# Three padding tiles move the weight buffers and the operands that meet them to other byte offsets

## The chip, the cores and the metric

One core of one Trainium2 chip runs the whole program in one launch. The metric is the device time of one execution in microseconds. Before the change it is 1166.29 us, the median of 3 runs (1164.71 to 1167.49). TensorE (PE in the profile) multiplies matrices, ScalarE (ACT) and VectorE (DVE) work element by element, GpSimd (POOL) does small things, and SyncE (SP) issues the weight loads.

## The reference

One layer on 256 tokens of width 2048. A combined projection of the normalised input feeds three branches, whose gated outputs are merged and projected:

```python
def hybrid_layer(x, mem, norm_g, w_in, ...):
    h = rms_norm(x, norm_g)
    proj = h @ w_in                                   # 2048 -> 16512 columns
    (aq, ak, av, az, br, bk, bv, bz, bwd, bad, cq, cz, ga, gb, gc) = jnp.split(proj, offsets, axis=-1)
    ya = chunked_band_attention(rms_norm(aq), rms_norm(ak), av, a_rel_bias) * jax.nn.silu(az)
    yb = rwkv7_time_mix(br, bk, bv, bwd, bad, ...) * jax.nn.silu(bz)
    mk, mv = jnp.split(rms_norm(mem, mem_norm_g) @ w_mem_kv, 2, axis=-1)
    yc = memory_cross_attention(rms_norm(cq), rms_norm(mk), mv) * jax.nn.silu(cz)
    merged = (jax.nn.sigmoid(ga) * (ya @ w_up_a) + jax.nn.sigmoid(gb) * (yb @ w_up_b)
              + jax.nn.sigmoid(gc) * (yc @ w_up_c))
    return x + merged @ w_o
```

All of it is float32. Nearly all of the arithmetic is in the products with weights: `w_in`, `w_mem_kv`, the three `w_up` and `w_o`.

## The kernel before

**The weight stream.** All weights are laid out in HBM as 185 chunks of 128 partitions by 2048 floats, in the order in which they are used. `wload` (L170) loads a chunk of 1 MB into `raw` (two buffers). `wchunk` (L183) turns each half of it into two tiles of the type float32r: ScalarE copies it to `whi` (L191), which rounds, and VectorE writes the rest, `raw - whi`, to `wlo` (L193). There are four buffers of each. Activations are split in the same way into a high and a low tile: `mh`, `ml` (the memory tokens), `xh`, `xl` (the input), `yth`, `ytl` (the outputs of branches A and C), `yh`, `yl` (of branch B) and `gh`, `gl` (the merged branches).

**The products.** Each product is three matmuls, high by high, low by high and high by low. A matmul has a stationary operand, which a weight load (LDWEIGHTS, PEld in the profile) puts into the array, and a moving operand, which streams through it. There are two forms.
- `proj` (L197; `proj_last`, L220, for the last output block) keeps the activations stationary, 128 columns at a time, and lets 512 columns of the weights stream: L210, L211 and L215, twelve matmuls to one half of a chunk.
- `proj_cm` (L251) is the other way round: 128 columns of the weights are stationary and 256 columns of the activations stream (L259, L260, L262).

Each matmul has a weight load of its own, as no two neighbours share the stationary operand. In a row of the profile such as `pp<-whi,xh` the names are the accumulator and the two operands.

**The order.** The order is that of the code. `spawn` and `tick` let the small work (attention, the RWKV recurrence, transposes) run as generators that take a step after every few matmuls. These small matmuls (L344, L493 and others) have ordinary float32 operands, not float32r.

**Where a tile lies.** A tile lies at the same byte offset in each of the 128 partitions. Pools hand out offsets one after another, in steps of 32 bytes, some from the left end of the partition and some (`side="right"`) from the right end. So an unused tile moves all that is handed out behind it. In the pools `const` (vectors and constants), `wts` (`raw`, `whi`, `wlo`) and `small` the order is const, wts, small, and behind them comes `xT` (`xh`, `xl`) and all else on the left. Buffers of one pool, and the columns that a matmul takes of a tile, are multiples of 512 bytes apart for all operands named above, so an operand's offset modulo 256 is the same in all its matmuls.

Of the kernel before, what the change touches and what calls it, by code (L numbers as in the profile page):

```python
# [18 lines left out]
P = 128  # L19
# [71 lines left out]
def build(nc, tc, A, out, dbg=None):  # L91
    dbg = dbg or {}
    ctx = ExitStack()
    with ctx:
        _build(ctx, nc, tc, A, out, dbg)


def _build(ctx, nc, tc, A, out, dbg):
    uid = [0]

    def nm(s):
        uid[0] += 1
        return f"{s}_{uid[0]}"

    def pool(st, name, bufs=1, side=None, space=None):
        kw = {}
        if side:
            kw["side"] = side
        if space is not None:
            kw["space"] = space  # L110
        return st.enter_context(tc.tile_pool(name=name, bufs=bufs, **kw))
# [3 lines left out]
    cp = pool(ctx, "const")  # L115
    wp = pool(ctx, "wts")
    sm = pool(ctx, "small")
# [4 lines left out]
    def t(pl, shape, tag, dtype=F32, bufs=1):  # L122
        return pl.tile(shape, dtype, name=nm(tag), tag=tag, bufs=bufs)
# [141 lines left out]
        return acc  # L265


    vec = t(cp, [P, NV], "vec")
    cst = t(cp, [P, NCST], "cst")
    ident = cst[:, C_ID:C_ID + P]  # L270
# [119 lines left out]
            yield 1  # L390


    xp = ExitStack()
    xpool = pool(xp, "xT")
    xh = t(xpool, [P, 16, S], "xh", F32R)
    xl = t(xpool, [P, 16, S], "xl", F32R)

    yc_st = ExitStack()
    ycp = pool(yc_st, "yc", side="right")
    ych = t(ycp, [P, 8, S], "yth", F32R)  # L400
# [722 lines left out]
```

## Time and profile before

| | |
|---|---|
| median of 3 runs | 1166.29 us |
| the profiled execution | 1162.67 us, of which the span from first to last instruction is 1160.9 |
| PE busy | 1141.2 us (98%), 6610 matmuls |
| PEld busy | 961.0 us (83%), beside PE |
| DVE, ACT, POOL busy | 804.7 (69%), 528.9 (46%), 167.5 (14%) |
| granted TensorE clock | 0.998 of 2.4 GHz on average |
| DMA | 212.75 MB, 183 GB/s on average |

PE's busy time is the union of matmuls that overlap, since a matmul is in flight longer (390 ns and more for 512 columns) than the distance at which the next one starts. So neither busy time nor the mean duration of a matmul says how fast TensorE gets on: that is read from the start times of neighbours in the timeline, and called spacing below.

### The profile page before, as it was taken

What the parts mean: (1) busy time and instruction counts of PE and PEld (TensorE: products, weight loads), DVE (VectorE), ACT (ScalarE), POOL (GpSimd) and SP (SyncE); (2) the same over time, 40 slices, a digit from 0 to 9 for tenths busy, and PEclk for the clock granted to TensorE, in tenths of its full rate; (3) what the DMA queues carried; (4) which work ended last, traced back from release to release, by engine and by line L of the source; (5) the groups of instructions that cost most, each with busy time, mean ns of one, the idle gap of its engine ahead of it and who ended that gap; (6) DMA issues with size and microseconds to landing.
All of it is one profiled execution on the core that took longest, in us unless ns stands there. A gap on an engine that the chain in (4) does not pass through costs nothing.

```text
span 1160.9 us, 16874 instructions
## 1 busy us (share of the span) xinstructions
PE 1141.2 (98%) x6610; PEld 961.0 (83%) x6610; DVE 804.7 (69%) x1378; ACT 528.9 (46%) x655; POOL 167.5 (14%) x232
## 2 busy tenths in 40 slices
PE   7999999999999999999999989899999999999998
PEld 6888989889889778988997779787788877888887
DVE  6874566556869667979786778956687956557443
ACT  6764545443643434444553634642553443444332
POOL 0100000034010204010214110213201203300000
PEclk9999999999999999999999999999999999999999
DMA  7765535466474654464644355554355574554663
GB/s 266 245 227 203 186 137 181 155 200 208 154 241 151 203 184 145 167 203 170 204 160 145 111 178 205 165 179 148 128 195 199 185 233 145 195 196 159 230 236 109
DMA packets 36905, 212.75 MB, mean 183 GB/s; under 512 B 5086, under 2 KB 7390, under 8 KB 13274
## 3 DMA queue, kind: packets, MB, share of 16 engines
q1 hardware_dynamic: 29664, 198.59, 49.9%
q0 software_dynamic: 3936, 9.44, 3.0%
q10 hardware_dynamic: 3226, 3.65, 1.0%
q8 instruction: 52, 0.85, 0.3%
q14 instruction: 27, 0.22, 0.1%
HBM read 206.95 MB, written 3.67 MB: 181 GB/s over the span
## 4 chain that ended last, share of the span: by engine, by line
PE 82%; DVE 9%; DMA 4%; issue 2%; ACT 1%; POOL 1%; SPq 0%; ACTq 0%; POOLq 0%; DVEq 0%
PE pp L210 21%; PE pp L211 20%; PE pp L215 20%; PE pp L259 4%; PE pp L260 4%; PE pp L262 4%; DVE wlo L193 3%; DMA raw<-in_wstream_dram 3%; DVE Xu L743 1%; DVE tmu L741 1%; DMA Tu<-scrt 1%; PE pp L232 1%; PE pp L234 1%; PE pp L231 1%; ACT whi L191 1%
## 5 line engine op out<-in xcount | busy, mean ns | idle before, releaser
L193 DVE TENSOR_TENSOR wlo<-raw,whi 128x1024 fp32r<-128x1024 f32 x368 | 455.8, 1250 | 255.4 <-ACT whi L191 254.3
L191 ACT CAST whi<-raw 128x1024 fp32r<-128x1024 f32 x368 | 380.2, 1051 | 533.4 <-PE pp L211 230.4
L210 PE MATMUL pp<-whi,xh 128*128 128x512 f32 x768 | 309.2, 403 | 1.5 <-ACT whi L191 1.5
L211 PE MATMUL pp<-whi,xl 128*128 128x512 f32 x768 | 300.8, 392 | 0.0
L215 PE MATMUL pp<-wlo,xh 128*128 128x512 f32 x768 | 206.6, 391 | 3.9 <-DVE wlo L193 3.9
L210 PEld LDWEIGHTS pp<-whi,xh 128*128 128x128 f32 x768 | 144.5, 188 | 35.8 <-ACT whi L191 3.0
L215 PEld LDWEIGHTS pp<-wlo,xh 128*128 128x128 f32 x768 | 144.2, 188 | 36.0 <-DVE wlo L193 5.9
L211 PEld LDWEIGHTS pp<-whi,xl 128*128 128x128 f32 x768 | 144.9, 189 | 28.6 <-issue 0.5
L259 PE MATMUL pp<-xh,whi 128*128 128x256 f32 x528 | 131.3, 287 | 0.0
L260 PE MATMUL pp<-xl,whi 128*128 128x256 f32 x528 | 129.6, 284 | 0.0
L259 PEld LDWEIGHTS pp<-xh,whi 128*128 128x128 f32 x528 | 101.2, 192 | 1.1 <-issue 0.6
L260 PEld LDWEIGHTS pp<-xl,whi 128*128 128x128 f32 x528 | 101.4, 192 | 0.6 <-issue 0.2
L262 PE MATMUL pp<-xh,wlo 128*128 128x256 f32 x528 | 74.1, 283 | 0.0
L262 PEld LDWEIGHTS pp<-xh,wlo 128*128 128x128 f32 x528 | 68.1, 192 | 0.0
L210 PE MATMUL pp<-whi,mh 128*128 128x512 f32 x128 | 50.9, 397 | 3.8 <-ACT whi L191 2.0
L210 PE MATMUL pp<-whi,yth 128*128 128x512 f32 x128 | 51.9, 405 | 0.0
L211 PE MATMUL pp<-whi,ytl 128*128 128x512 f32 x128 | 50.5, 395 | 0.0
L211 PE MATMUL pp<-whi,ml 128*128 128x512 f32 x128 | 50.1, 391 | 0.2 <-DVE ml L309 0.2
L741 DVE TENSOR_TENSOR tmu<-Tu,Xu 128x112 f32<-128x112 f32 (+29 forms) x124 | 32.6, 263 | 13.5 <-DMA Tu<-scrt 10.4
L210 PE MATMUL pp<-whi,gh 128*128 128x512 f32 x96 | 37.5, 390 | 0.0
L211 PE MATMUL pp<-whi,gl 128*128 128x512 f32 x96 | 37.4, 389 | 0.0
L215 PE MATMUL pp<-wlo,yth 128*128 128x512 f32 x128 | 35.0, 396 | 0.0
(258 smaller groups left out, 1346.3 us busy)
## 6 DMA issues: line engine op xcount, KB each, us to landing
raw<-in_wstream_dram SPq DMA_DIRECT2D x184, 1024.0 KB, 5.0
xraw<-in_xT_dram SPq DMA_DIRECT2D x8, 256.0 KB, 4.8
Tu<-scrt POOLq DMA_DIRECT2D x4, 512.0 KB, 4.6
xr<-in_x_dram POOLq DMA_DIRECT2D x8, 256.0 KB, 5.3
xraw<-in_memT_dram SPq DMA_DIRECT2D x7, 256.0 KB, 5.6
out_dram<-xr POOLq DMA_DIRECT2D x6, 256.0 KB, 3.4
bias<-in_rel_dram POOLq DMA_DIRECT2D x4, 256.0 KB, 3.7
tmpA<-in_bc_dram ACTq DMA_DIRECT2D x8, 128.0 KB, 4.3
```

The lines of the kernel that those rows point to most:

```text
L191: SC.copy(hi, sl)
L193: V.tensor_tensor(out=lo, in0=sl, in1=hi.bitcast(F32), op=ALU.subtract)
L210: T.matmul(acc[tt], xh[:, kt + k2, sl], hv[:, k2], start=(kt + k2 == 0), stop=False)
L211: T.matmul(acc[tt], xl[:, kt + k2, sl], hv[:, k2], start=False, stop=False)
L215: T.matmul(acc[tt], xh[:, kt + k2, sl], lv[:, k2], start=False, stop=(last and k2 == 1))
L231: T.matmul(acc, xh[:, kt + k2, sl], hv[:, k2, cs], start=(kt + k2 == 0), stop=False)
L232: T.matmul(acc, xl[:, kt + k2, sl], hv[:, k2, cs], start=False, stop=False)
L234: T.matmul(acc, xh[:, kt + k2, sl], lv[:, k2, cs], start=False, stop=(kt + k2 == nk - 1))
L259: T.matmul(acc, hv[:, k2], xh[:, kt + k2, :], start=(kt + k2 == 0), stop=False)
L260: T.matmul(acc, hv[:, k2], xl[:, kt + k2, :], start=False, stop=False)
L262: T.matmul(acc, lv[:, k2], xh[:, kt + k2, :], start=False, stop=(kt + k2 == 15))
L741: V.tensor_tensor(out=tv, in0=Tu[:, s, s + 1:32].unsqueeze(2).to_broadcast([P, n, m]), in1=X[:, s:s + 1, 0:m].to_broadcast([P, n, m]), op= ...
```

## The change

Three tiles that nothing reads or writes are added: 96 bytes at the head of `const`, 64 bytes at the end of `small`, and 32 bytes at the right end of the partition, ahead of the pool of `yth` and `ytl`.

```diff
+    t(cp, [P, 24], "padw")
     vec = t(cp, [P, NV], "vec")
     cst = t(cp, [P, NCST], "cst")
 ...
+    t(sm, [P, 16], "padx")
     xp = ExitStack()
     xpool = pool(xp, "xT")
     xh = t(xpool, [P, 16, S], "xh", F32R)
     xl = t(xpool, [P, 16, S], "xl", F32R)
 
+    padp = pool(ctx, "padr", side="right")
+    t(padp, [P, 8], "padr")
     yc_st = ExitStack()
     ycp = pool(yc_st, "yc", side="right")
     ych = t(ycp, [P, 8, S], "yth", F32R)
```

In the built programs the instructions of every engine are the same, in the same order, with the same shapes, waits and semaphore updates. What differs is the byte offsets. Modulo 256 they are:

| tiles | before | after |
|---|---|---|
| `raw`, `whi`, `wlo` | 160 | 0 |
| `xh`, `xl`, `mh`, `ml`, `gh`, `gl`, `yh`, `yl` | 160 | 64 |
| `xraw`, `merged`, `vL` and other tiles of the left side | 160 | 64 |
| `yth`, `ytl`, `mkT`, `mv`, `cqT` | 224 | 192 |
| the RWKV tiles `AX`, `BK`, `Tu`, `Xu` | 224 | 192 |
| `cst` (identity, masks), `eye8`, `warm` | 0 | 96 |
| the RWKV tiles `w2a2`, `rk0` | 0 | 224 |

So where a weight tile meets `xh`, `mh`, `gh` or `yh`, the two offsets are 160 and 160 before, and 0 and 64 after. Where it meets `yth` they are 160 and 224 before, and 0 and 192 after.

## Rows read from the trace of the kernel before

**Rows 1.** The profiled page: busy us (share of the span) xinstructions
```profile
PE 1141.2 (98%) x6610; PEld 961.0 (83%) x6610; DVE 804.7 (69%) x1378; ACT 528.9 (46%) x655; POOL 167.5 (14%) x232
```

**Rows 2.** The page's chain that ended last, by engine
```profile
PE 82%; DVE 9%; DMA 4%; issue 2%; ACT 1%; POOL 1%; SPq 0%; ACTq 0%; POOLq 0%; DVEq 0%
```

**Rows 3.** Waits of PE: engine line waited for: us in total, times, longest
```profile
PE pp L215 <- DVE wlo L193: 3.9, 3, 2.8
PE pp L210 <- ACT whi L191: 3.5, 2, 2.0
```

**Rows 4.** Waits of all engines, same columns
```profile
DVE wlo L193 <- ACT whi L191: 254.3, 174, 5.7
ACT whi L191 <- PE pp L211: 230.4, 138, 4.4
ACT whi L191 <- DMA raw<-in_wstream_dram: 213.9, 76, 8.7
```

**Rows 5.** Groups by shape: line engine op out<-in xcount | busy, mean ns | idle before
```profile
L210 PE MATMUL pp<-whi,xh 128*128 128x512 f32 x768 | 309.2, 403 | 1.5 <-ACT whi L191 1.5
L259 PE MATMUL pp<-xh,whi 128*128 128x256 f32 x528 | 131.3, 287 | 0.0
L210 PE MATMUL pp<-whi,yth 128*128 128x512 f32 x128 | 51.9, 405 | 0.0
L210 PE MATMUL pp<-whi,mh 128*128 128x512 f32 x128 | 50.9, 397 | 3.8 <-ACT whi L191 2.0 <-ACT mh L308 0.9 <-ACT whi L451 0.9
L210 PE MATMUL pp<-whi,gh 128*128 128x512 f32 x96 | 37.5, 390 | 0.0
L210 PE MATMUL pp<-whi,yh 128*128 128x512 f32 x64 | 25.2, 394 | 0.0
L231 PE MATMUL pp<-whi,gh 128*128 128x256 f32 x32 | 8.3, 282 | 0.0
L231 PE MATMUL pp<-whi,gh 128*128 128x512 f32 x16 | 6.3, 392 | 0.0
```

**Rows 6.** Timeline of PE, `proj` on `xh`: start us, us, engine line op xcount
```profile
880.11 0.39 PE L210 MATMUL pp<-whi,xh 128*128 128x512 f32 x1
880.34 0.39 PE L211 MATMUL pp<-whi,xl 128*128 128x512 f32 x1
...
881.47 1.07 PE L215 MATMUL pp<-wlo,xh 128*128 128x512 f32 x4
882.38 0.39 PE L210 MATMUL pp<-whi,xh 128*128 128x512 f32 x1
```

**Rows 7.** Timeline of PE, `proj` on `yth`
```profile
890.62 0.40 PE L210 MATMUL pp<-whi,yth 128*128 128x512 f32 x1
890.86 0.39 PE L211 MATMUL pp<-whi,ytl 128*128 128x512 f32 x1
891.09 0.40 PE L210 MATMUL pp<-whi,yth 128*128 128x512 f32 x1
...
893.42 0.40 PE L210 MATMUL pp<-whi,yth 128*128 128x512 f32 x1
```

**Rows 8.** Timeline of PE, from `proj` to `proj_cm`, and on in it
```profile
257.67 1.07 PE L215 MATMUL pp<-wlo,xh 128*128 128x512 f32 x4
258.58 0.28 PE L259 MATMUL pp<-xh,whi 128*128 128x256 f32 x1
258.69 0.28 PE L260 MATMUL pp<-xl,whi 128*128 128x256 f32 x1
...
259.77 0.28 PE L259 MATMUL pp<-xh,whi 128*128 128x256 f32 x1
...
260.49 0.88 PE L262 MATMUL pp<-xh,wlo 128*128 128x256 f32 x6
```

**Rows 9.** Timeline of PE, two runs of float32 matmuls
```profile
58.68 1.03 PE L344 MATMUL ps<-cst,qn 128*128 128x128 f32 x8
147.91 3.62 PE L493 MATMUL ps<-mkT,cqT 128*128 128x256 f32 x16
```

**Rows 10.** Groups: one of the float32 matmuls, and the two casts
```profile
L493 PE MATMUL ps<-mkT,cqT 128*128 128x256 f32 x32 | 7.2, 379 | 0.0
L344 PE MATMUL ps<-cst,qn 128*128 128x128 f32 x64 | 8.3, 273 | 0.0
L191 ACT CAST whi<-raw 128x1024 fp32r<-128x1024 f32 x368 | 380.2, 1051 | 533.4 <-PE pp L211 230.4 <-DMA raw<-in_wstream_dram 213.9 <-PE pp L260 39.2
L193 DVE TENSOR_TENSOR wlo<-raw,whi 128x1024 fp32r<-128x1024 f32 x368 | 455.8, 1250 | 255.4 <-ACT whi L191 254.3
```

**Rows 11.** The page's DMA issues: op xcount, KB each, us to landing
```profile
raw<-in_wstream_dram SPq DMA_DIRECT2D x184, 1024.0 KB, 5.0
```

## The prediction

> **What bounds the kernel now.** I read the page's busy shares first: TensorE is busy 98% of the span, the next engine 69% [rows 1]. Then what TensorE waits for: 3.9 us for `wlo` and 3.5 us for `whi` in 1160.9 [rows 3], while ScalarE waits 230.4 us for TensorE to free a `whi` buffer [rows 4]. So the weight feed is ahead, and the time is the sum of the distances at which matmuls start. The chain agrees with a reservation: 82% of it is PE, and 13% is DVE and DMA, places where the feed or the RWKV chain sets the pace [rows 2].
>
> Busy means of single matmuls (403 ns) overlap and say nothing of the spacing, so I read that from start times in the timeline.
> - `proj` on `xh`: ten matmuls from 880.11 to 882.38, 2.27/10 = 227 ns [rows 6].
> - `proj` on `yth`: twelve from 890.62 to 893.42, 2.80/12 = 233.3 ns, alternately about 240 and 230 as printed [rows 7].
> - `proj_cm`: six from 259.77 to 260.49, 120 ns [rows 8].
> - float32 matmuls of 256 columns: 16 in 3.62 us, (3.62 - 0.379)/15 = 216 ns; of 128 columns: (1.03 - 0.273)/7 = 108 ns [rows 9, 10].
>
> Two sizes give a slope and a fixed part. float32r: (227 - 120)/256 = 0.418 ns a column, so 107 ns for 256 columns and 214 for 512, and a fixed part of 13 ns for each matmul. float32: 108/128 = 0.84 ns a column, twice the slope, with a fixed part of 0 to 2 ns. All of them have a weight load each. And the `yth` matmuls, same shape and same moving tiles, have a fixed part of 19 ns. What differs there is the stationary offset, 224 where `xh` has 160. So the fixed part of a float32r matmul depends on where its operands lie; that is the one quantity which this change can move.
>
> **The change part by part.** No instruction, wait or order changes, so nothing is queued behind anything new. The three tiles cost no instruction. What is left is four kinds of access at new offsets.
>
> *float32r matmuls.* Each count is that of the high-by-high line times three lines. On `xh`, `mh`, `gh`, `yh`: (768 + 128 + 96 + 64 + 16) x 3 = 3216 with 512 columns. On `yth`: 128 x 3 = 384. With 256 columns: (528 + 32) x 3 = 1680 [rows 5]. In all 5280. The trace of before holds the offset pairs (160, 160) and (160, 224), and not (0, 64) or (0, 192), so the new fixed part is bounded from both sides. The low end is that of float32, 2 ns [rows 9]. The high end is that of `yth`, 19 ns [rows 7], for the new pairs too are 64 apart modulo 128. Within a stage the fixed part is not always 13: the first `proj_cm` matmul after a `proj` stage has a spacing of 0.11 us, a fixed part of 3 to 6, before 0.12 sets in [rows 8]. So 13 is not a floor of the float32r form; it comes from how the moving reads and the weight load fall on each other. Before, both offsets are odd multiples of 32 bytes; after, both are multiples of 64, a kind of pair that no row shows. I take 6 ns, the row nearest between the ends (107 + 6 = 113, which prints as 0.11). Gain: 7 ns x (3216 + 1680) = 34.3 us, and (19 - 6) x 384 = 5.0 us for `yth`, in all 39.3 us.
>
> Of this I let 85% reach the end, since 82% of the chain is PE [rows 2] and the stages in which something else sets the pace don't gain: 33.4 us. The feed covers the rest: a chunk is 24 matmuls, 24 x 0.220 = 5.28 us instead of 24 x 0.227 = 5.45, against 2 x 1.051 us on ScalarE, 2 x 1.250 us on VectorE [rows 10] and 5.0 us to land with two buffers in flight [rows 11]. What would be late next is the `raw` load, by way of VectorE, which has to free the buffer.
>
> *Casts and weight DMA.* ScalarE and VectorE read `raw` at 0 instead of 160, and DMA writes it there. No row shows what an offset does to them. Bound: TensorE waits 7.4 us for both casts [rows 3], so no more than that can be won; a loss would first use up ScalarE's 230.4 us of waiting [rows 4]. I take 0.
>
> *float32 matmuls.* There are 6610 - 5280 = 1330 records [rows 1]. Their fixed part is 0 to 2 ns at the pairs that `L344` (identity at 0, `qn` at 160) and `L493` (224 and 224) have [rows 9], so offsets have not mattered to them. I take 0; at the worst they would get the 13 ns of the others, 1330 x 11 = 15 us.
>
> *Element-wise work.* RWKV and attention tiles move by 32, 96 or 160 bytes; hidden as long as TensorE is 98% busy, 0.
>
> The sum against the profiled execution, 1162.67 us (span 1160.9): 1162.67 - 33.4 = 1129.3. The median of the runs shown lies 3.6 us above that execution, so the forecast is 1133 us on the median's scale.
>
> **What the skill says.** The rows have `yth` 6 ns slower than `xh` for nothing but its offset [rows 6, 7]. The Trainium skill, "TensorE: Matmul & The Clock Gate", "Step-by-step: what each phase is for", says that the moving operand and the weight load have two independent read ports, so that loading the next weights takes nothing from the running matmul; "SBUF — State Buffer", "SBUF: two separate sides", that PE never waits on another engine's port. By that an offset could not matter and the change would do nothing, a rival below; this trace does not agree, as 19 is not 13.
> The same TensorE page, "Wait — 56ns, not 53.3ns?", gives a spacing of N/2.4 + 2.5 ns at full clock, 215.8 for 512 columns. Only the float32 rows here are that close to their slope. An estimate by it: 11 ns off each of 4896 and 17 off each of 384, some 60 us, the floor among the rivals.
>
> **The rivals.**
> - *Floor.* The new offsets take away the whole collision, and float32r gets the fixed part of float32, 2 ns [rows 9]: 11 x 4896 + 17 x 384 = 60.4 us, of which 51 at 85%: 1115; all of it, 1106. For it: the float32 matmuls have weight loads too and no such cost. Against: they stream at half the pace, so they leave more room.
> - *Only the distance counts.* What matters is the difference of the two offsets, and 64 is the slow one. Then every matmul on `xh`, `mh`, `gh`, `yh` gets what `yth` has, 6.3 ns more: 3216 x 6.3 = 20.3 us, TensorE being the bound almost throughout: 1186; if the 256-column ones pay it too, another 10.6 us, 1197. For it: this is the only dependence that the trace shows directly. Against: it says nothing of why the pair (160, 160), with no distance at all, costs 13 ns. It decides as soon as the mean spacing on `xh` exceeds 227 ns.
> - *Nothing, or `yth` alone.* The 13 ns belong to the form, and only `yth`, whose tiles now have the offset distance of -64, changes: at most 384 x 6.3 = 2.4 us, so 1164 to 1166. For it: in all stages on `mh`, `xh`, `gh` the spacing is 227, however different the work beside them. Against: the 0.11 us at a stage's start [rows 8]. That the change doesn't do what it says is this case too: offsets move, and the array doesn't notice.
>
> **How the numbers follow.** Forecast 36%, floor 20%, distance 32%, nothing or `yth` alone 12%. Faster by over 0.2% (2.3 us, about what a measurement of this kernel can tell from none) are the forecast, the floor and a sixth of the last: 0.58. Slower is the distance: 0.32. The same: 0.10. The signs are mixed, so the range has to reach across: from 1104, the floor with all of it passed on, to 1190, the distance paid by the wide matmuls with 4 us for the unknown offsets of the casts. It leaves out the distance paid in full (about 8%) and a little below. The forecast's own range is 1120 to 1145, from a fixed part of 3 ns to one of 9.
>
> **What would show it.** In the profile after: the spacing of `L210` and `L211` on `xh` (220 ns if right, 216 by the floor, 233 by the distance, 227 by nothing), of `L259` (113, 109, up to 126, 120), and of `yth` equal to that of `xh`. The float32 rows stay at 216 and 108. TensorE's waits for `wlo` and `whi` grow from 7.4 us if the feed takes part of the gain. The prediction is wrong if the spacing rises, or if it falls and the span doesn't; a changed duration of the casts with unchanged spacing would mean that I looked at the wrong access.

## The result, and the profile after

The changed kernel takes 1173.44 us, the median of 4 runs (1171.67 to 1176.71), against 1165.5 us (1164.5 to 1167.49) for the kernel before, run beside it. The ratio is 1.0083, with a 95% interval of 1.0063 to 1.0104: it is slower by 0.8%, which is 9.7 us (7.3 to 12.1). The forecast, 1133 us, had the wrong sign.

The profiled execution took 1176.71 us, with a span of 1174.9 where before has 1160.9. Its page, first the busy shares (as [rows 1]), then the chain (as [rows 2]), the two casts (as [rows 10]) and the weight load (as [rows 11]):

```profile
PE 1156.2 (98%) x6610; PEld 959.5 (82%) x6610; DVE 805.1 (69%) x1378; ACT 529.3 (45%) x655; POOL 167.7 (14%) x232
...
PE 87%; DVE 6%; DMA 3%; ACT 1%; issue 1%; POOL 1%; SPq 0%; ACTq 0%; DVEq 0%; POOLq 0%
...
L193 DVE TENSOR_TENSOR wlo<-raw,whi 128x1024 fp32r<-128x1024 f32 x368 | 455.7, 1249 | 268.9 <-ACT whi L191 266.1
L191 ACT CAST whi<-raw 128x1024 fp32r<-128x1024 f32 x368 | 380.1, 1049 | 548.1 <-PE pp L211 262.5
...
raw<-in_wstream_dram SPq DMA_DIRECT2D x184, 1024.0 KB, 5.0
```

PE is busy 15.0 us longer with the same 6610 matmuls, the weight loads 1.5 us less, and every other engine as long as before, to 0.5 us. The casts and the weight load take what they took. TensorE's waits for the weights, as in [rows 3] (engine, line, what it waited for: us in total, times, longest):

```profile
PE pp L215 <- DVE wlo L193: 3.6, 3, 2.7
...
PE pp L210 <- ACT whi L191: 3.4, 2, 1.9
```

That is 7.0 us against 7.4. The casts, as in [rows 4], wait longer for TensorE and less for DMA:

```profile
DVE wlo L193 <- ACT whi L191: 266.1, 177, 5.6
ACT whi L191 <- PE pp L211: 262.5, 146, 4.6
ACT whi L191 <- DMA raw<-in_wstream_dram: 189.2, 72, 8.7
```

ScalarE's wait for a `whi` buffer grew from 230.4 to 262.5 us. So the feed is as far ahead as it was, and TensorE itself is slower. The timeline of PE in the changed kernel (start us, us, line, operands, count) shows at which matmuls: `proj_cm`, `proj` on `xh` and `proj` on `yth`, where [rows 8, 6, 7] show them before.

```profile
263.14 0.28 PE L259 MATMUL pp<-xh,whi 128*128 128x256 f32 x1
263.26 0.28 PE L260 MATMUL pp<-xl,whi 128*128 128x256 f32 x1
...
265.02 0.28 PE L262 MATMUL pp<-xh,wlo 128*128 128x256 f32 x1
...
888.86 0.39 PE L210 MATMUL pp<-whi,xh 128*128 128x512 f32 x1
889.09 0.40 PE L211 MATMUL pp<-whi,xl 128*128 128x512 f32 x1
...
890.73 0.86 PE L215 MATMUL pp<-wlo,xh 128*128 128x512 f32 x3
...
900.00 0.39 PE L210 MATMUL pp<-whi,yth 128*128 128x512 f32 x1
...
902.75 0.39 PE L210 MATMUL pp<-whi,yth 128*128 128x512 f32 x1
```

- `proj_cm`: 16 matmuls from 263.14 to 265.02, 117.5 ns each, where it was 120.
- `xh`: 8 from 888.86 to 890.73, 234 ns, where it was 227.
- `yth`: 12 from 900.00 to 902.75, 229 ns, where it was 233.3.

The means over all neighbours of a family, taken from the start times of the whole trace with pauses left out, give the account (a family has its high and its low tile):

| matmuls | count | before, ns | after, ns | change, us |
|---|---|---|---|---|
| on `xh`, `mh`, `gh`, `yh`, 512 columns | 3216 | 227.7 | 233.3 | +18.0 |
| on `yth`, 512 columns | 384 | 233.4 | 229.3 | -1.6 |
| `proj_cm`, 256 columns | 1584 | 119.9 | 117.8 | -3.3 |
| last block, 256 columns | 96 | 119.5 | 113.8 | -0.5 |
| sum | | | | +12.6 |

The spans differ by 14.0 us. The rest is about the clock: the mean granted clock of the execution is 0.996, and 0.998 before, which makes, as an estimate, 1174.9 x 0.004 - 1160.9 x 0.002 = 2.4 us. The windows show two places where the array now runs for a while at 1.2 of its 2.4 GHz and before did not. One lies between 700 and 800 us (mean clock 0.98, before 1.00), the other at the start (columns: stretch; its us, busy us and instructions of PE, PEld, VectorE, ScalarE and GpSimd, the granted clock, DMA share, GB/s). After:

```profile
14.00:16.00 2.00, 0.68 (x3) 0.20 (x2) 0.88 (x3) 1.43 (x2) 0.00 (x0) 1.00 0.99 244
16.00:18.00 2.00, 1.38 (x6) 1.16 (x7) 1.97 (x4) 2.00 (x4) 0.00 (x0) 1.00 0.89 319
18.00:20.00 2.00, 2.00 (x7) 1.52 (x6) 2.00 (x4) 1.12 (x3) 0.00 (x0) 0.51 0.79 280
20.00:22.00 2.00, 2.00 (x8) 1.58 (x7) 1.00 (x3) 0.55 (x1) 0.00 (x0) 0.63 0.84 269
```

Before, the same stretches:

```profile
14.00:16.00 2.00, 1.01 (x5) 0.51 (x3) 0.92 (x3) 1.05 (x2) 0.00 (x0) 1.00 0.83 267
16.00:18.00 2.00, 1.00 (x4) 0.86 (x5) 1.93 (x3) 2.00 (x4) 0.00 (x0) 1.00 0.92 317
18.00:20.00 2.00, 2.00 (x10) 1.65 (x9) 2.00 (x4) 1.51 (x4) 0.00 (x0) 1.00 0.66 243
```

In both, TensorE works 2.0 to 2.1 us of the 4 ahead of it (0.68 + 1.38, and 1.01 + 1.00); the clock falls to 0.51 in the one and stays at 1.00 in the other. This part does not belong to the offsets: in the last experiment below, whose matmuls on `mh` lie as before, the clock falls in the same stretch (0.57 from 18 to 20 us), and another execution of the changed kernel had a mean clock of 1.000 and a span of 1169.9, where 1160.9 - 2.3 + 12.6 = 1171.2 would be expected.

The float32 matmuls are where they were [rows 9]: eight in 1.03 us, though the distance of their operands (stationary less moving offset; here the identity moves) went from 160 to -32, and sixteen in 3.61, where both stay at one offset. In the fourteen traces of this document, which have distances of 0, 64, 160 and 224 modulo 256 there, the spacing of these transposes (the first 14 neighbours of each trace) is 108.8 to 109.1 ns.

```profile
60.70 1.03 PE L345 MATMUL ps<-cst,qn 128*128 128x128 f32 x8
...
151.23 3.61 PE L497 MATMUL ps<-mkT,cqT 128*128 128x256 f32 x16
```

### The profile page after: what moved, and what is told of

Its sections match the earlier page's. It is cut to its first block, busy times and chain, and to the rows that moved or that the text cites. A ratio compares the mean times of both kernels' runs of the same rounds, so it can differ in the third digit from the quotient of the medians.

```text
span 1174.9 us, 16874 instructions
## 1 busy us (share of the span) xinstructions
PE 1156.2 (98%) x6610; PEld 959.5 (82%) x6610; DVE 805.1 (69%) x1378; ACT 529.3 (45%) x655; POOL 167.7 (14%) x232
## 4 chain that ended last, share of the span: by engine, by line
PE 87%; DVE 6%; DMA 3%; ACT 1%; issue 1%; POOL 1%; SPq 0%; ACTq 0%; DVEq 0%; POOLq 0%
PE pp L210 22%; PE pp L211 21%; PE pp L215 21%; PE pp L259 5%; PE pp L260 5%; PE pp L262 5%; DMA raw<-in_wstream_dram 3%; DVE wlo L193 2%; PE pp L232 1%; PE pp L234 1%; PE pp L231 1%; ACT whi L191 1%; PE ps L532 1%; PE ps L497 1%; PE ps L709 1%
## 5 line engine op out<-in xcount | busy, mean ns | idle before, releaser
L193 DVE TENSOR_TENSOR wlo<-raw,whi 128x1024 fp32r<-128x1024 f32 x368 | 455.7, 1249 | 268.9 <-ACT whi L191 266.1
L191 ACT CAST whi<-raw 128x1024 fp32r<-128x1024 f32 x368 | 380.1, 1049 | 548.1 <-PE pp L211 262.5
L210 PE MATMUL pp<-whi,xh 128*128 128x512 f32 x768 | 312.8, 407 | 1.5 <-ACT whi L191 1.5
L211 PE MATMUL pp<-whi,xl 128*128 128x512 f32 x768 | 304.5, 396 | 0.0
L215 PE MATMUL pp<-wlo,xh 128*128 128x512 f32 x768 | 211.1, 396 | 3.6 <-DVE wlo L193 3.6
L215 PEld LDWEIGHTS pp<-wlo,xh 128*128 128x128 f32 x768 | 144.2, 188 | 40.0 <-DVE wlo L193 5.3
L210 PEld LDWEIGHTS pp<-whi,xh 128*128 128x128 f32 x768 | 145.1, 189 | 38.6 <-ACT whi L191 2.8
L211 PEld LDWEIGHTS pp<-whi,xl 128*128 128x128 f32 x768 | 145.1, 189 | 32.4 <-issue 0.5
L259 PE MATMUL pp<-xh,whi 128*128 128x256 f32 x528 | 129.2, 283 | 0.0
L260 PE MATMUL pp<-xl,whi 128*128 128x256 f32 x528 | 127.4, 280 | 0.0
L259 PEld LDWEIGHTS pp<-xh,whi 128*128 128x128 f32 x528 | 99.1, 188 | 1.1 <-issue 0.6
L260 PEld LDWEIGHTS pp<-xl,whi 128*128 128x128 f32 x528 | 99.1, 188 | 0.6 <-issue 0.2
L210 PE MATMUL pp<-whi,mh 128*128 128x512 f32 x128 | 52.4, 409 | 2.9 <-ACT whi L191 1.9
L211 PE MATMUL pp<-whi,ml 128*128 128x512 f32 x128 | 51.2, 400 | 0.2 <-DVE ml L310 0.2
L210 PE MATMUL pp<-whi,yth 128*128 128x512 f32 x128 | 51.3, 401 | 0.0
L211 PE MATMUL pp<-whi,ytl 128*128 128x512 f32 x128 | 50.1, 392 | 0.0
L210 PE MATMUL pp<-whi,gh 128*128 128x512 f32 x96 | 37.9, 395 | 0.0
L211 PE MATMUL pp<-whi,gl 128*128 128x512 f32 x96 | 37.8, 394 | 0.0
L215 PE MATMUL pp<-wlo,mh 128*128 128x512 f32 x128 | 35.9, 402 | 0.0
```

Source lines behind the costliest of these rows:

```text
L191: SC.copy(hi, sl)
L193: V.tensor_tensor(out=lo, in0=sl, in1=hi.bitcast(F32), op=ALU.subtract)
L210: T.matmul(acc[tt], xh[:, kt + k2, sl], hv[:, k2], start=(kt + k2 == 0), stop=False)
L211: T.matmul(acc[tt], xl[:, kt + k2, sl], hv[:, k2], start=False, stop=False)
L215: T.matmul(acc[tt], xh[:, kt + k2, sl], lv[:, k2], start=False, stop=(last and k2 == 1))
L259: T.matmul(acc, hv[:, k2], xh[:, kt + k2, :], start=(kt + k2 == 0), stop=False)
```

## The experiments

Four theories went into them. **A**: the spacing of a float32r matmul is set by the distance of the stationary from the moving operand, modulo 256. **B**: by the weights' own offset. **C**: what stands behind it is a collision of the next weight load with the reads of the running matmul. **D**: the 13 ns are the form's own. Ratios are against the kernel before, run beside each; a kernel without one was run once. Spacings are means over a trace as above.

### One padding tile at a time

The weights' tile alone (weights and left side to offsets 0 and 0, `yth` as before at 224):

```diff
+    t(cp, [P, 24], "padw")
     vec = t(cp, [P, NV], "vec")
```

> Padding for the weights alone: weight tiles at 0 modulo 256 as after, and xh, mh, gh, yh at 0 too (distance 0 as before); yth 480 past the weights modulo 512 (-32). Theory A, only the distance of the two operands' offsets counts: spacing on xh, mh, gh, yh 227 ns, proj_cm 120 ns, as before, and the time that of before within 3 us (yth has a distance that no run had, 227 to 236). Theory B, the weights' own offset counts (a multiple of 256 is the slow place): spacing 233 on xh, and about 1173 us as after.

Measured: ratio 1.0005 (0.9989 to 1.002). The trace, `proj` on `xh`, 6 matmuls in 1.36 us, 227 ns:

```profile
881.35 0.39 PE L210 MATMUL pp<-whi,xh 128*128 128x512 f32 x1
...
882.71 0.39 PE L210 MATMUL pp<-whi,xh 128*128 128x512 f32 x1
```

All families have their spacing of before (227.2 to 227.7, `yth` 233.2, `proj_cm` 119.9). The weights' offset went from 160 to 0 and nothing moved.

The operands' tile alone (weights at 160, left side at 224):

```diff
+    t(sm, [P, 16], "padx")
     xp = ExitStack()
```

> The 64 bytes ahead of xh alone: weight tiles at 160 as before, xh, mh, gh, yh and yth all 64 past them. Theory A (distance): xh, mh, gh, yh 233.3 ns, proj_cm 118 ns, the 256-column matmuls of the last block 113 ns, all as after, and yth 233.3 as before; so 1.6 us above after, about 1175 us. Theory B (weights' own offset): xh 227, proj_cm 120, the time of before, 1165.5.

Measured: 1174.01 us, ratio 1.0077 (1.0049 to 1.0105), as the whole change. The trace, 6 matmuls in 1.40 us, 233 ns:

```profile
890.15 0.39 PE L210 MATMUL pp<-whi,xh 128*128 128x512 f32 x1
...
891.55 0.39 PE L210 MATMUL pp<-whi,xh 128*128 128x512 f32 x1
```

`proj_cm` has 117.8 and the last block 113.8, to the tenth the values after the whole change, with both operands 160 bytes further on modulo 256. A stands, B is refuted; of the alignment to 64, which the forecast went by, nothing is left. One rival is left by these two, the activations' own offset: 160 and 0 have given 227, 64 and 224 have given 233. It falls with the first kernel of the next section, where `mh` lies at 160 as before, the weights at 0, and the spacing is 233.4.

### A map of the distances

Two kernels give each family a distance of its own, by tiles like those above of other lengths (in floats), the weights at 0:

```diff
+    t(cp, [P, 24], "padw")
...
+    t(sm, [P, 32], "padx")                # [P, 8] in the second
...
+    t(padp, [P, 32], "padr")              # 24
...
+    t(mp, [P, 8], "padm")                 # 16, ahead of mh
...
+    t(gp, [P, 16], "pady")                # 48, ahead of yh
...
+    t(gp, [P, 16], "padg")                # 16, ahead of gh
```

> Weight tiles at 0, and one distance for each family: xh 128, mh 160, yh 192, gh 256, yth 352 (modulo 512). If the distance counts modulo 128, xh and gh have 227 ns as at 0, and yh 233 as at 64. If modulo 256, gh has 227, yh the 229 that yth has at 448 after, and yth what 96 gives. If modulo 512 or not periodic, gh and yh differ from those. Some distance may give less than 227, down to 216, the spacing of the float32 matmuls; theory B has 233 for all of them.

> Weight tiles at 0, and five more distances: xh 32, mh 96, yh 224, gh 288, yth 384 (modulo 512). Modulo 128: xh and gh equal, mh and yh equal, yth 227. Modulo 256: gh equal to xh, yth equal to the 128 of the other probe. Theory B has 233 ns for all of them. The proj_cm matmuls, where the weights are stationary, have the distance with the other sign.

Measured: 1174.99 and 1172.29 us. In the first, `yh` lies at 192 and `gh` at 256:

```profile
1039.84 0.39 PE L210 MATMUL pp<-whi,yh 128*128 128x512 f32 x1
...
1042.58 0.39 PE L210 MATMUL pp<-whi,yh 128*128 128x512 f32 x1
...
1100.90 0.39 PE L210 MATMUL pp<-whi,gh 128*128 128x512 f32 x1
...
1103.62 0.39 PE L210 MATMUL pp<-whi,gh 128*128 128x512 f32 x1
```

Twelve matmuls in 2.74 us (228) and twelve in 2.72 (227). So 256 is as good as 0, and 192 lies between. With the other kernels below, the means in ns by distance (stationary less moving, modulo 256):

| distance | 0 | 32 | 64 | 96 | 128 | 160 | 192 | 224 |
|---|---|---|---|---|---|---|---|---|
| 512 columns | 227.2 | 233.2 | 233.3 | 234.2 | 232.5 | 233.4 | 229.1 | 233.2 |
| 256 columns | 119.9 | 118.9 | 114.1 | 118.2 | 119.5 | 120.0 | 117.8 | 116.7 |

The 256-column value at 32 is from the last block, the others are from `proj_cm`. Three distances were run with the weights at 0 and at 160, and the two agree within 0.2 ns at 512 columns: 96, 160 and 192. The period is 256: buffers fix the distance modulo 512, and its upper half repeats the lower within 0.2 ns (256 gives 227.2, 288 gives 233.1, 352 gives 234.2, 384 gives 232.3, 448 gives 229.3, 480 gives 233.2). The two rows do not run together: the best distance for 512 columns is nearly the worst for 256.

A mean can hide two paces. At 64 bytes and 256 columns (the kernel of "Distances chosen by family") `proj_cm` has 22 runs of 16 or more neighbours without another matmul between them; 16 go at 113.3 to 114.0 ns, 6 at 117.8, and 114.1 is the mean of both.

### Below 32 bytes

Tiles 64 columns longer, used from a column other than 0: `xh` and `mh` 16 bytes from the weights, `gh` 8, `yh` 4.

```diff
-    xh = t(xpool, [P, 16, S], "xh", F32R)
+    xh = t(xpool, [P, 16 * S + 64], "xh", F32R)[:, 4:4 + 16 * S].rearrange("p (a b) -> p a b", b=S)
...
-    yh = t(gp, [P, 8, S], "yh", F32R)
+    yh = t(gp, [P, 8 * S + 64], "yh", F32R)[:, 1:1 + 8 * S].rearrange("p (a b) -> p a b", b=S)
```

> Distances under 32 bytes, by slices of tiles that are 256 bytes longer: xh and mh 16 past the weights modulo 256, gh 8, yh 4, yth 64 as before. If the collision is decided by 16-byte or smaller pieces, mh and xh have about 233, as at 32, and gh and yh lie between 227 and 233. If by 32-byte pieces or larger, all four stay at 227. Theory D has no reason for any change. In proj_cm the distance is -16 (120 at 0, 117 at -32).

Measured: 1170.37 us; 233.3 ns on `mh`, 231.1 on `xh`, 230.6 on `gh`, 232.3 on `yh`, and 117.6 in `proj_cm` (119.9 before). One float of distance costs 5 ns at 512 columns. But 231.1 is the pace of no run: `xh` lies 16 bytes from the weights as `mh` does, and of the 82 runs of its 512-column matmuls that nothing interrupts, 34 go at 227 ns and 48 at 233, none at both (the first two matmuls of a run left out). Two stretches of twelve:

```profile
232.02 0.39 PE L210 MATMUL pp<-whi,xh 128*128 128x512 f32 x1
...
234.74 0.39 PE L210 MATMUL pp<-whi,xh 128*128 128x512 f32 x1
...
847.73 0.40 PE L210 MATMUL pp<-whi,xh 128*128 128x512 f32 x1
...
850.53 0.40 PE L210 MATMUL pp<-whi,xh 128*128 128x512 f32 x1
```

They take 2.72 and 2.80 us, with the same operands at the same offsets. So distance does not settle the spacing by itself everywhere; what settles the pace when a run starts is open.

### High and low tile at different distances

`xl` lies 64 bytes further than `xh`, so that neighbouring weight loads differ. (Two more tiles, not shown, keep `mh`, `yh` and `gh` at distance 0.)

```diff
     xh = t(xpool, [P, 16, S], "xh", F32R)
+    t(xpool, [P, 16], "padl")
     xl = t(xpool, [P, 16, S], "xl", F32R)
```

> xl alone is moved 64 bytes (distance 64), xh, mh, yh, gh at 0, yth at 64 as before. Theory C with the next load: after L210 (during which xl is loaded, at distance 64) the spacing rises to 233 or more, after L211 (next load xh, distance 0) it stays near 227, and the low weights' matmuls (L215, xh alone) stay at 227. If the matmul's own stationary operand counts, L211 rises in place of L210. If the mean of a pair is what locks, both are near 230.

Measured: 1165.32 us. On `xh` and `xl` the most frequent spacings run in a cycle of 226, 236, 231 and 227, mean 230.0; the matmuls of L215, which use `xh` alone, have 227 to 228; the other 512-column families are as before, and `proj_cm`, where `xl` is now at -64, has 118.4. After L210 the mean is 230.0 and after L211 232.5, so neither reading that names one of the two came out; the pair as a whole rises.

### Half weight loads

In `proj` the low-part matmul loads 64 columns instead of 128; the other 64 rows of its products are left out.

```diff
+                        sl = slice(tt * P, tt * P + 64)
-                        T.matmul(acc[tt], xl[:, kt + k2, sl], hv[:, k2], start=False, stop=False)
+                        T.matmul(acc[tt][:64], xl[:, kt + k2, sl], hv[:, k2], start=False, stop=False)
```

> The low-by-high matmuls (L211) of proj take 64 stationary columns in place of 128, so each of their weight loads reads half as much; the low parts of tokens 64 to 127 and 192 to 255 are left out. All offsets as before. Theory C, the 13 ns come from the next weight load colliding with the moving reads: the matmul during which the half load runs, the high-by-high one ahead of it (L210), is followed sooner, 216 to 222 ns in place of 227, and the one after stays at 227. Theory D, the 13 ns are the form's own: 227 everywhere. If the load of the same matmul counts, the L211 spacing falls in place of that of L210.

Measured: 1172.01 us. The trace on `gh` (128*64 is the half load):

```profile
1094.95 0.39 PE L210 MATMUL pp<-whi,gh 128*128 128x512 f32 x1
1095.18 0.40 PE L212 MATMUL pp<-whi,gl 128*64 128x512 f32 x1
...
1096.34 0.85 PE L216 MATMUL pp<-wlo,gh 128*128 128x512 f32 x3
```

Six in 1.39 us, 232 ns. Over the trace it is 228.8 after a full matmul, while the half load runs, 232.9 after a half one, while a full load runs, and 230.0 to 230.3 in a family's mean (families at distance 0): slower than with full loads throughout. A collision whose price goes with the bytes loaded would have made it faster, so that form of C falls for 512 columns. To see whether this comes from the alternation, all loads but those that open a product or close it were halved, in `proj` and in `proj_cm`:

```diff
+                w = P if kt == 0 or last else 64
...
-                        T.matmul(acc[tt], xh[:, kt + k2, sl], hv[:, k2], start=(kt + k2 == 0), stop=False)
+                        T.matmul(acc[tt][:w], xh[:, kt + k2, sl], hv[:, k2], start=(kt + k2 == 0), stop=False)
...
+                w = P if kt + k2 == 0 else 64
-                T.matmul(acc, hv[:, k2], xh[:, kt + k2, :], start=(kt + k2 == 0), stop=False)
+                T.matmul(acc[:w], hv[:, k2, :w], xh[:, kt + k2, :], start=(kt + k2 == 0), stop=False)
```

> All offsets as before. But for the first and the last group of each accumulation, every float32r matmul of proj and proj_cm takes 64 stationary columns in place of 128, so all the weight loads are of one size, half as long; most of the products of half of the output rows are left out. Theory C (the fixed part is made by the weight load beside the moving reads): spacing well under 227 and 120, near 220 and 113 or at the float32 form's 216 and 109. Theory D (the form's own): 227 and 120 as before.

Measured: 1162.51 us. `proj` has 230 to 231 ns (single values from 224 to 236). `proj_cm` falls from 119.9 to 113.7:

```profile
263.93 0.28 PE L261 MATMUL pp<-xh,whi 128*64 128x256 f32 x1
...
265.74 0.28 PE L261 MATMUL pp<-xh,whi 128*64 128x256 f32 x1
```

Sixteen in 1.81 us, 113 ns, at distance 0, where full loads take 120. So D is wrong for 256 columns, as the 114.1 of full loads at distance 64 says too. That the load takes this time from the matmul beside it is not shown: a matmul with a half load is itself half as wide, and in the trace the spacing goes more with that. A half matmul is followed after 113.5 ns when the load beside it is a full one (33 cases), a full matmul after 117.1 when the load beside it is a half one (33), and after 118.6 to 119.2 when it is full (46). For 512 columns a smaller load at distance 0 costs time instead; what is shown is that the size of the stationary operand matters, not how.

In `proj_cm`, contrary to the section on the products, the neighbours L259 and L260 do share their stationary operand (`hv[:, k2]`). Each has its own load all the same (PE and PEld both count 6610), and before the spacing is 119.9 ns after L259, with the operand kept, and 119.8 from L260 to L259, with a new one.

### Distances chosen by family

Two of the map's findings can be put to use. `xh` serves both forms; at 192 it should lose 1.4 ns on 512 columns and win 5.8 on 256. `mh` and `gh` stay at 0, and `yth` goes to 0.

```diff
+    t(sm, [P, 48], "padx")
...
+    t(padp, [P, 16], "padr")
...
+    t(mp, [P, 16], "padm")
...
+    t(gp, [P, 16], "pady")
```

> Weight tiles stay at 160. Distance 0 modulo 256 for mh, yh, gh and now yth too; xh 192 past the weights, so that in proj_cm, where the weights are stationary, they are 64 past the moving operand, the distance at which the 256-column matmuls of the last block had 114 ns. By distance alone: yth 227 (384 x 6.1 = 2.3 us less than before), proj_cm 114 (1584 x 6 = 9.5 us less), proj on xh 229.2 (2304 x 1.5 = 3.4 us more): 8.4 us less than before, near 1157, faster than both kernels. If 256 columns behave in proj_cm by another rule than in the last block (proj_cm 118 to 120): 1 to 2 us more than before.

Measured: 1161.83 us, median of 12 (1154.56 to 1164.76), against 1164.61, ratio 0.9969 (0.995 to 0.9988). It beats both kernels, by less than expected: 3.6 us by the ratio, where 8.4 were expected. Three of the twelve times, 1154.56 to 1155.86, hold all of it; the other nine lie at 1161.34 to 1164.76. The spacings are as expected: `xh` 229.2, `proj_cm` 114.1, `yth` 227.5, the rest 226.9 to 227.6. The trace, `proj_cm` (24 in 2.72 us, 113 ns) and `yth` (8 in 1.81 us, 226 ns):

```profile
259.91 0.28 PE L259 MATMUL pp<-xh,whi 128*128 128x256 f32 x1
...
262.63 0.28 PE L259 MATMUL pp<-xh,whi 128*128 128x256 f32 x1
...
891.53 0.39 PE L210 MATMUL pp<-whi,yth 128*128 128x512 f32 x1
...
893.34 0.39 PE L215 MATMUL pp<-wlo,yth 128*128 128x512 f32 x1
```

By spacing it should win 1584 x 5.8 = 9.2 us on `proj_cm` and 384 x 5.9 = 2.3 on `yth`, and lose 2304 x 1.4 = 3.2 on `xh`: 8.3 in all. The profiled execution, at the slow end of the twelve with a span of 1163.0, shows where these can go. TensorE's waits over the whole span:

```profile
PE pp L215 <- DVE wlo L193: 5.9, 5, 2.8
PE pp L210 <- ACT whi L191: 5.1, 3, 2.8
...
PE pp L262 <- DVE wlo L193: 1.2, 2, 0.8
```

That is 12.2 us against 7.4 [rows 3], and 4.0 of the 4.8 more lie between 360 and 420 us (5.5 against 1.5), the end of a `proj_cm` stage and what follows. The clock is the other part (windows, columns as above):

```profile
390.00:394.00 4.00, 2.60 (x12) 1.80 (x10) 0.00 (x0) 0.00 (x0) 0.00 (x0) 1.00 1.04 270
394.00:398.00 4.00, 2.57 (x7) 2.00 (x8) 2.36 (x2) 2.46 (x3) 0.00 (x0) 0.71 0.14 55
398.00:402.00 4.00, 4.00 (x17) 3.23 (x16) 2.36 (x2) 1.53 (x2) 0.00 (x0) 0.86 0.79 262
```

From 390 to 394 us ScalarE and VectorE stand still with DMA at full share, TensorE runs out of weights and works 2.60 us of 4, and then its clock falls to a mean of 0.71. Its longest wait there is 2.8 us. The kernel before runs out in the same place, for 1.5 us, and its clock stays:

```profile
390.00:394.00 4.00, 2.57 (x12) 1.79 (x10) 0.00 (x0) 1.05 (x2) 0.00 (x0) 1.00 0.82 259
394.00:398.00 4.00, 3.95 (x17) 3.26 (x18) 3.16 (x3) 2.83 (x3) 0.00 (x0) 1.00 0.25 49
```

Over the execution the clock is 0.994 against 0.998, 1163.0 x 0.006 - 1160.9 x 0.002 = 4.7 us. So -8.3 + 4.8 + 4.7 = +1.2, near the 2.1 us by which this span exceeds that of before. Only this execution has a profile; how much of it holds for the other eleven is open.

### Narrow matmuls at other distances, and `yth` alone

In the first two kernels two more tiles, not shown, keep `mh`, `yh` and `gh` at distance 0.

```diff
+    t(sm, [P, 40], "padx")                # xh at 160, narrow at 96; [P, 24] in the second: 96 and 160
...
+    t(padp, [P, 16], "padr")              # yth at 0
```

> mh, yh, gh, yth at distance 0; xh 160 past the weights, so in proj_cm the stationary weights are 96 past the moving operand. By the map of distances xh in proj has 233.4 ns and the four other families 227. For 256 columns 96 has not been run: by the neighbours (64: 114, 128: 119.5) between 114 and 120.

> As the run before with xh 96 past the weights: proj on xh 234.2 ns, and proj_cm at 160, not run yet; by the neighbours (128: 119.5, 192: 117.8) 117 to 120.

Measured: 1168.99 and 1176.71 us; `xh` 233.4 and 234.2 ns, `proj_cm` 118.2 and 120.0, `yth` 227.9 and 227.8. They fill the last places of the map.

With the right-hand tile alone, `yth` meets the weights at distance 0 and nothing else moves:

```diff
+    padp = pool(ctx, "padr", side="right")
+    t(padp, [P, 16], "padr")
```

> Only yth and ytl are moved, by 64 bytes on the right side, to distance 0 from the weights: 227 ns in place of 233.3 for 384 matmuls, 2.3 us less than before (ratio 0.998), all other spacings as before. If the distance were not what counts for yth, no change.

Measured: 1162.73 us against 1163.94, ratio 0.9993 (0.9979 to 1.0008), so no gain that the times can tell. In the trace twelve matmuls take 2.73 us, 227.5 ns:

```profile
889.38 0.39 PE L210 MATMUL pp<-whi,yth 128*128 128x512 f32 x1
...
892.11 0.39 PE L210 MATMUL pp<-whi,yth 128*128 128x512 f32 x1
```

Before [rows 7] they took 2.80. The 6 ns that `yth` paid were its distance.

## Why the prediction was wrong

- **What bounds the kernel.** Right. PE stays at 98%, the feed waits for it longer than before, and a spacing that rose by 12.6 us in the sum, with about 2.4 us of clock, came out as 14.0 us of span in the profiled pair. The times have 9.7 us (7.3 to 12.1), near the 85% passed on, which would be 10.7.
- **That an operand's place moves the spacing.** Right, and nothing else that the offsets could reach moved. That the spacing splits into 0.418 ns a column and one fixed part for both sizes was not: at distance 64 the same arithmetic gives (233.3 - 113.8) / 256 = 0.467 ns a column and -5.7 ns.
- **"I take 6 ns, the row nearest between the ends."** This is the step that failed. It read the rows as alignment: both offsets are multiples of 64, so a better kind of pair. The first tile's experiment moves both from odd multiples of 32 to multiples of 256 and leaves 227 ns; the second leaves both at odd multiples of 32 and gives the 233 of the change. Distance is what counts, and the change takes it from 0 to 64, one of the slow ones. In place of 7 ns less, 3216 matmuls got 5.6 ns more. In the prediction's terms the fixed part that it put at 6 for all came out at 19 for these (233.3 - 214), 15 for `yth`, 11 for `proj_cm` (117.8 - 107) and 7 for the last block, where it fits by luck.
- **The 0.11 us row as its evidence** [rows 8]. It did show that 120 is not the least for 256 columns: whole runs have 113 to 114 with half loads, and with full ones at distance 64. It said nothing of offsets, since it and the 0.12 behind it have the same ones, and nothing of 512 columns.
- **`yth`, 13 ns less.** It gained 4.1, as its distance went from 64 to 192, which for 512 columns lies between. The prediction called both new pairs "64 apart modulo 128"; the period is 256, and 64 and 192 give 233.3 and 229.1.
- **"Only the distance counts".** The rival was right in mechanism, and its first term in size: 6.3 ns and 20.3 us forecast on 3216 matmuls, 5.6 and 18.0 measured; its time, 1186, was 13 us too long. Its reading of `yth` as unchanged and its second term, 10.6 us on the 256-column matmuls, were not: these fell by 2.1 to 5.7 ns, 3.8 us. What was held against it, that distance 0 still costs 13 ns, was no objection: 0 is one distance among others, and for 256 columns 64 takes 6 ns off it.
- **Casts, weight DMA, float32 matmuls, element-wise work at 0.** Right: 1049 and 1249 ns [rows 10], 5.0 us [rows 11], 1.03 and 3.61 us [rows 9].
- **The two ports.** The Trainium skill, "TensorE: Matmul & The Clock Gate", "Step-by-step: what each phase is for", lets a weight load take nothing from the running matmul. The runs disagree more plainly than the trace before did: with the same shapes and loads, the distance of the operand that is loaded from the one that streams moves the spacing between 227.2 and 234.2 ns and between 113.8 and 120.0, and one float of it makes 5 ns. The prediction noted the disagreement and then trusted its own guess at what removes it.

So the cause of the slowdown is shown down to the distance of the two operands. Open is why 227 is the least for 512 columns while 256 columns have theirs at distance 64, why one distance can have two paces, and what in the chip has a period of 256 bytes. That load and reads collide (C) is argued from the two operands' part in it, not shown. No run here separates a bank of memory from a read unit.

## What to carry to other kernels

Where TensorE is the bound and each matmul has its own weight load, read the spacing from start times, and compare families by the distance of their two operands' offsets modulo 256, each column count for itself. Look at runs and not only at means, as one distance can have two paces. Count on part of a gain: of 12.6, 14.2 and 8.3 us by spacing the times showed 9.7, 9.0 and 3.6 (the change, the operands' tile alone, the distances by family). A padding tile of a few bytes is a cheap sweep, but make it a sweep: the one pair that two rows suggest is a guess. And a dependence which the trace shows directly (`yth` against `xh`, same shape, another distance) is to be weighed above a pattern that one's own arithmetic suggests (multiples of 64).

## What the runs showed of the hardware

- The mean spacing of float32r matmuls repeats with 256 bytes of distance and spreads over 227 to 234 ns for 512 columns and 114 to 120 for 256, whatever the absolute offsets, as far as tried; 4 bytes of distance already cost 5 ns at 512 columns.
- At one distance there can be two paces, each kept by a whole run: 227 and 233 ns at 16 bytes and 512 columns, 113 to 114 and 117.8 at 64 bytes and 256 columns.
- A stationary operand of 64 columns in place of 128 takes 6 ns off a 256-column matmul and adds 3 to a 512-column one at distance 0.
- Float32 matmuls of the same kernel show no such dependence: those of 128 columns have 108.8 to 109.1 ns at distances of 0, 64, 160 and 224.
- A feed that falls behind can cost twice: a wait of 2.8 us was followed by a mean clock of 0.71 over 4 us and 0.86 over the next 4. A wait of 1.5 us in the same place of the kernel before was not.
